# The first chunk of columns for both token tiles, unit by unit: a two-layer hybrid trunk on one core

## The chip, the core and the metric

The kernel runs on one core of a Trainium2 chip. A core has TensorE (PE: matmuls; its weight loads are shown as PEld), VectorE (DVE), ScalarE (ACT), GpSimd (POOL) and SyncE (SP, which here issues the DMAs). The metric is the device time of one execution in microseconds, the median of several runs. Before the change it is 1353.75 us, of 3 runs from 1353.36 to 1354.12.

## The reference

The input x is 256 tokens by 1024 features, float32. Two layers follow; each is a SwiGLU feed-forward, a mixing sub-layer (differential attention beside an mLSTM, gated and merged) and a second SwiGLU, each between two RMS norms:

```
h = rmsnorm(x, ffn1_norm_pre[l])
x = x + 0.5 * rmsnorm(swiglu(h, ffn1_w_gu[l], ffn1_w_down[l]), ffn1_norm_post[l])
...                                # mixing, then the second feed-forward
swiglu(h, w_gu, w_down):  g, u = split(h @ w_gu);  return (silu(g) * u) @ w_down
```

Only the very first feed-forward's first products, and the store of the last result, are touched here. Its w_gu is 1024 by 5632, its w_down 2816 by 1024.

## The kernel before, in words

**Tiling.** The tokens are two tiles of 128 (t = 0, 1). The contraction over 1024 features is eight k tiles of 128; k tiles 0 to 3 are group g = 0 and 4 to 7 are group g = 1. The columns of w_gu are taken in 11 chunks of 256 gate and 256 up columns, so one large product is 128x128 by 128x512. Every operand is in two parts, high and remainder, and a product is three matmuls (`mm3`, lines 453 to 462): high by high (L457), high of x by remainder of w (L459), remainder of x by high of w (L461). A chunk for one token tile is 8 x 3 = 24 matmuls, for both 48.

**Weights** come in units of 512 KB, [128, 1024] in SBUF; a unit of w_gu holds two k tiles of one chunk and is loaded by two DMAs of 256 KB. Units 0 to 3 are chunk 0, 4 to 7 chunk 1, 8 and 9 the first rows of w_down. `WeightStream` (lines 68 to 136) loads each into one of 5 buffers (`raw`), then splits it: a ScalarE cast (L111, `whi`) and a VectorE subtraction (L113, `wlo`), whole or in two halves of one k tile each. A unit's buffer is free for the load of the unit five later when its subtraction is done. `get` splits a unit at the latest when a product wants it; `tick` splits one more whenever PACE = 3600 ns of planned TensorE time have passed since the last tick that did so, at 216 ns for each large matmul.

**x's operand.** The first norm's weights are loaded as a row, `first_row`, and transposed to columns (L1080, L1081). For each token tile, `first` (lines 1043 to 1066) transposes x by groups of four k tiles into one PSUM bank (`transposes`, L357), multiplies the bank by the columns on VectorE (L341), casts on ScalarE (L334) and subtracts on VectorE (L336), 128x512 each. `inverse_rms` (L377, L383, L384) takes two squares on ScalarE and a power on GpSimd; its result is wanted only when a chunk is complete.

**Order.** TensorE's order is the order of the program text (`manual_schedule`). For ScalarE and VectorE the order is written only inside the block at lines 1077 to 1083, which covers token tile 0's `first`; elsewhere they, SP and GpSimd are ordered by a scheduler. `Flow` interleaves the large products with tasks: a task that waits for other engines is taken up again when a planned time has passed. In the first sub-layer `turns` gives chunk 0 as all eight k tiles of tile 0, then all eight of tile 1; tile 1's `first` is a task that begins 3000 ns of planned time after tile 0's (WAIT_FIRST). The first DMAs in SP's order: tile 0's first half, the row, tile 0's second half, units 0 to 3, tile 1 whole. When tile t of a chunk is complete, its `hidden` task (lines 502 to 513) runs: a Silu on ScalarE (L504, which brings a table load the first time), a product on VectorE (L507), two transpositions on TensorE (L511) some 18 products after the tile was complete, and a split.

`keep_busy` issues a few matmuls of nothing. PSUM has four banks `acc` (the down products' accumulators), two `mm` (a chunk's products) and two `tr` (transpositions). `new_ps` (line 492) gives a bank of `mm` when the first call covers all eight k tiles, otherwise one of `acc`.

**The end.** `Sublayer.finish` of the last sub-layer (lines 430 to 434) adds the normed result to x in two halves per token tile (L428) and stores each from SP (L433).

Of the kernel before, what the change touches and what calls it, by code (L numbers as in the profile page):

```python
# [20 lines left out]
T = 2  # L21
# [9 lines left out]
# ns of TensorE's time: a large product, a transposition; one split; what stages wait for  # L31
# [7 lines left out]
WAIT_FIRST = 3000  # L39
# [28 lines left out]
class WeightStream:  # L68
    """Weights in the order of their use: each unit of [128, 1024] is loaded, and split exactly
    into a float32r part and its float32r remainder. Loads run RAW_BUFS units ahead of the splits, the  # L70
    splits as far ahead of the products as there is room, one every PACE ns of products."""
# [27 lines left out]
    def split_parts(self, parts):  # L99
        """The next unit's split, in parts: stages"""  # L100
# [30 lines left out]
    def get(self, key, used):  # L131
        """The unit, of which a product is about to use so many elements"""
        i = self.index[key]
        self.split_to(i + 1)
        self.left[i] -= used
        return self.done[i]


class Flow:
    """The order of the instructions. The large products are the foreground; what hangs on other  # L140
    engines' results is a task, a generator that yields (its products' time, the time until its next
    stage can start), and is taken up between the large products when that time has passed."""
# [24 lines left out]
    def ran(self, n):  # L167
        """n large products have been issued."""
# [11 lines left out]
def kernel(ctx: ExitStack, tc: tile.TileContext, I, out):  # L180
# [42 lines left out]
    # k tiles a unit, and columns of a k tile  # L223
# [32 lines left out]
    x = const.tile([P, T, D], F32, name="x")  # L256
    first_row = const.tile([KD, P], F32, name="first_row")
    for hh in range(2):
        s = slice(512 * hh, 512 * hh + 512)
        nc.sync.dma_start(out=x[:, 0, s], in_=x_in[0, 0:P, s])  # L260
        if hh == 0:
            nc.sync.dma_start(out=first_row, in_=I["ffn1_norm_pre"][0].rearrange("(k p) -> k p", p=P))
    idle = w1.tile([P, 384], F32, tag="w1", name="idle")
    nc.vector.memset(idle, 0.0)
    W.load_to(4)
    nc.sync.dma_start(out=x[:, 1, :], in_=x_in[0, P:2 * P, :])
# [22 lines left out]
    def small_operands():  # L289
        """Per-feature vectors as columns, the lambdas, the gates' biases."""  # L290
# [17 lines left out]
        for l in range(L):  # L308
# [11 lines left out]
            # the negative of lambda  # L320
# [5 lines left out]
    def row(ap, nm):  # L326
        """A row vector of 1024, on every partition."""
# [4 lines left out]
    def split_out(dst_h, dst_l, src, ns):  # L332
        """Stages: src in two parts"""
# [4 lines left out]
    def columns_split_out(dst_h, dst_l, src, w, nm):  # L338
        """The same of src [128, 4, 128] times a column of w [128, 4] for each"""
# [20 lines left out]
    def transposed(src, xT, nm):  # L360
        """Stages: src [128, 1024] -> its split, transposed operand."""
# [10 lines left out]
    def squares(src, scale, nm, halves):  # L372
        """The sum of the squares of each half of src * scale"""
# [16 lines left out]
    class Sublayer:  # L390
        """What the norms between two sub-layers hold."""

        def __init__(self, i, post, pre):
            self.post_row, self.pre_row = post, pre
            self.nm = f"s{i + 1}"
            self.ahead = AHEAD if i >= 0 else 0

# [15 lines left out]
        def half(self, t, y, hh, scale):  # L413
            """y's half hh is complete."""
# [5 lines left out]
        def finish(self, t):  # L420
            """x += y * rsqrt * post; the next operand from it"""
# [8 lines left out]
            if self.pre is None:  # L430
                for s in hs:
                    update(s)
                    nc.sync.dma_start(out=out[0, t * P:(t + 1) * P, s], in_=x[:, t, s])  # L433
                return
# [18 lines left out]
    def mm3(ps, s, w, first, last):  # L453
        """ps += s.T @ w, of operands in two parts each."""
# [9 lines left out]
    def new_y(nm):  # L464
        """[128, 1024] in halves"""
        return [acc.tile([P, 512], F32, tag="acc", name=f"{nm}_{hh}") for hh in range(2)]

    def dense(y, s, w, first, last, halves=(0, 1)):
        """y += one k tile's product"""
# [4 lines left out]
    def dense_tail(ys, n, ks, operand, weights, prepare, half, finish):  # L474
        """The last k tiles, one token tile and one half after the other."""
# [8 lines left out]
    def turns(c, ahead):  # L484
        """The order in chunk c of a sub-layer: token tile, 1 for the chunk after it, k tiles. While the second token
        tile isn't there yet, the next chunk is begun."""
# [638 lines left out]
```

## Time and profile before

| | before |
|---|---|
| median of 3 runs | 1353.75 us (1353.36 to 1354.12) |
| the profiled execution: span | 1351.6 us |
| median minus span | 2.15 us |
| PE busy | 1338.9 us, 99% |
| ACT busy / DVE busy | 697.7 us, 52% / 858.7 us, 64% |
| DMA | 242.25 MB, mean 179 GB/s |

The span is from the first to the last instruction of the one profiled execution; the runs are timed from outside, which puts some 2 us around it. PE's busy time counts a matmul until a modelled end, so matmuls overlap by it; the distance between the starts of two is what one costs. [...]

### The profile page before, as it was taken

Reading aid. Unit: us, or ns where it says so; the run is one execution under the profiler, and the core shown is the slowest. Engines: PE = TensorE matmul, PEld = TensorE weight load, DVE = VectorE, ACT = ScalarE, POOL = GpSimd, SP = SyncE. Lnnn points to the kernel's source line nnn. Section 1 sums busy time; section 2 is a strip of 40 time slices with the busy share of each in tenths; the row PEclk is TensorE's granted clock in tenths of the full one; section 3 lists DMA queues with packets and bytes.
Section 4 is the critical chain, followed back from the end, with each engine's and each line's share of the span. In section 5 each row is a group of like instructions: output and inputs, shape, how many; then the busy total and the mean of one; then the engine's idle time right before and its main releaser. Section 6 shows DMA issues by size and latency. Waiting matters only on the chain.

```text
span 1351.6 us, 17400 instructions
## 1 busy us (share of the span) xinstructions
PE 1338.9 (99%) x6320; PEld 1094.8 (81%) x6320; DVE 858.7 (64%) x1245; ACT 697.7 (52%) x1063; POOL 56.2 (4%) x77
## 2 busy tenths in 40 slices
PE   8999999999999999999999999999999999999998
PEld 6888888788888888888888888887788888888886
DVE  6555566879785676555585555658887656755553
ACT  6444455567454465444464444555674444644442
POOL 1000000000000010000010000100001000100000
PEclk9999999999999999999999999999999999999999
DMA  8765659575667567555565555595664765555560
GB/s 292 246 188 187 187 156 199 147 159 118 144 187 205 175 198 228 185 186 188 180 208 185 185 186 182 164 208 122 152 161 105 206 208 174 191 184 186 186 191 32
DMA packets 160105, 242.25 MB, mean 179 GB/s; under 512 B 14250, under 2 KB 108564, under 8 KB 160020
## 3 DMA queue, kind: packets, MB, share of 16 engines
q1 hardware_dynamic: 160020, 241.15, 61.7%
q8 instruction: 49, 0.80, 0.2%
q14 instruction: 36, 0.29, 0.1%
HBM read 240.06 MB, written 1.05 MB: 178 GB/s over the span
## 4 chain that ended last, share of the span: by engine, by line
PE 94%; DVE 2%; DMA 1%; POOL 1%; issue 1%; ACT 0%; SPq 0%; DVEq 0%; POOLq 0%; ACTq 0%
PE gu L459 12%; PE gu L457 12%; PE gu L461 12%; PE y L457 6%; PE y L461 6%; PE y L459 6%; PE in_gl L461 2%; PE in_gl L459 2%; PE in_gl L457 2%; PE hp L511 1%; PE in_mv L461 1%; PE in_mv L459 1%; PE w_proj_m L457 1%; PE w_proj_a L457 1%; PE w_proj_m L459 1%; PE w_proj_a L461 1%
## 5 line engine op out<-in xcount | busy, mean ns | idle before, releaser
L113 DVE TENSOR_TENSOR wlo<-raw,whi 128x1024 fp32r<-128x1024 f32 (+2 forms) x443 | 535.8, 1217 | 254.2 <-ACT whi L111 239.4
L111 ACT CAST whi<-raw 128x1024 fp32r<-128x1024 f32 (+2 forms) x443 | 460.0, 1045 | 234.9 <-PE y L461 75.1
L459 PE MATMUL y<-wlo,hTh 128*128 128x512 f32 x352 | 142.2, 404 | 0.0
L457 PE MATMUL y<-whi,hTh 128*128 128x512 f32 x352 | 139.4, 396 | 0.0
L461 PE MATMUL y<-whi,hTl 128*128 128x512 f32 x352 | 139.2, 395 | 0.0
L457 PEld LDWEIGHTS y<-whi,hTh 128*128 128x128 f32 x352 | 66.2, 188 | 15.4
L461 PEld LDWEIGHTS y<-whi,hTl 128*128 128x128 f32 x352 | 66.4, 189 | 13.8
L459 PEld LDWEIGHTS y<-wlo,hTh 128*128 128x128 f32 x352 | 66.3, 188 | 13.7
L459 PE MATMUL gu<-wlo,x0Th 128*128 128x512 f32 x176 | 70.6, 401 | 1.0 <-DVE wlo L113 1.0
L457 PE MATMUL gu<-whi,x0Th 128*128 128x512 f32 x176 | 69.4, 394 | 1.1 <-ACT whi L111 0.7
L459 PE MATMUL gu<-wlo,s3xTh 128*128 128x512 f32 x176 | 69.7, 396 | 0.0
L459 PE MATMUL gu<-wlo,s2xTh 128*128 128x512 f32 x176 | 69.7, 396 | 0.0
L459 PE MATMUL gu<-wlo,s5xTh 128*128 128x512 f32 x176 | 69.6, 396 | 0.0
L461 PE MATMUL gu<-whi,x0Tl 128*128 128x512 f32 x176 | 69.1, 393 | 0.1
L457 PE MATMUL gu<-whi,s5xTh 128*128 128x512 f32 x176 | 68.8, 391 | 0.0
L457 PE MATMUL gu<-whi,s2xTh 128*128 128x512 f32 x176 | 68.8, 391 | 0.0
L457 PE MATMUL gu<-whi,s3xTh 128*128 128x512 f32 x176 | 68.8, 391 | 0.0
L461 PE MATMUL gu<-whi,s3xTl 128*128 128x512 f32 x176 | 68.7, 391 | 0.0
L461 PE MATMUL gu<-whi,s2xTl 128*128 128x512 f32 x176 | 68.7, 391 | 0.0
L461 PE MATMUL gu<-whi,s5xTl 128*128 128x512 f32 x176 | 68.7, 391 | 0.0
L334 ACT CAST hTh<-hp 128x256 fp32r<-128x256 f32 x88 | 32.4, 368 | 36.6 <-PE hp L511 36.6
L336 DVE TENSOR_TENSOR hTl<-hp,hTh 128x256 fp32r<-128x256 f32 x88 | 37.1, 421 | 7.3 <-ACT hTh L334 7.3
(455 smaller groups left out, 2604.3 us busy)
## 6 DMA issues: line engine op xcount, KB each, us to landing
raw<-in_ffn_w_gu_dram SPq DMA_DIRECT2D x352, 256.0 KB, 4.2
raw<-in_w_in_dram SPq DMA_DIRECT2D x124, 512.0 KB, 5.1
raw<-in_ffn_w_down_dram SPq DMA_DIRECT2D x88, 512.0 KB, 4.7
raw<-in_w_proj_a_dram SPq DMA_DIRECT2D x16, 512.0 KB, 4.0
raw<-in_w_proj_m_dram SPq DMA_DIRECT2D x16, 512.0 KB, 4.7
raw<-in_w_out_dram SPq DMA_DIRECT2D x16, 512.0 KB, 4.7
gb<-in_gate_b_dram SPq DMA_DIRECT2D x8, 256.0 KB, 5.3
raw<-in_w_in_dram SPq DMA_DIRECT2D x4, 384.0 KB, 7.0
```

The lines of the kernel that those rows point to most:

```text
L111: nc.scalar.copy(hi[:, c], raw[:, c])
L113: nc.vector.tensor_tensor(lo[:, c], raw[:, c], hi[:, c].bitcast(F32), op=ALU.subtract)
L334: nc.scalar.copy(dst_h, src)
L336: nc.vector.tensor_tensor(dst_l, src, dst_h.bitcast(F32), op=ALU.subtract)
L457: nc.tensor.matmul(ps, lhsT=sh, rhs=wh, start=first, stop=False)
L459: nc.tensor.matmul(ps, lhsT=sh, rhs=wl, start=False, stop=False)
L461: nc.tensor.matmul(ps, lhsT=sl, rhs=wh, start=False, stop=last)
L511: nc.tensor.transpose(out=pt[:, j, :], in_=hh[:, j * P:(j + 1) * P], identity=ident)
```

## The change

The first chunk of the first sub-layer gets an order of its own, `first_chunk`: a few k tiles of token tile 0, the same of tile 1, and so on, so that each unit of weights is used by both tiles before the next. It is inside a block in which ScalarE's and VectorE's order is the text's too. x is loaded in four halves, the first norm's row from ScalarE's queue. x's operand is made k tile by k tile: a ScalarE copy with a column scale (high) and one VectorE instruction for the remainder. Units 0 and 1 are split in halves between them; `first_weights` splits the next unit in halves. Both tiles' `inverse_rms` come near the end of the chunk. The last sub-layer's token tile 1 is updated and stored in four quarters, and the stores alternate between SP's and ScalarE's queues. (Comment lines and docstrings of the file are emptied; line numbers after the edits differ.)

```diff
-    for hh in range(2):
+    def x_half(t, hh):
         s = slice(512 * hh, 512 * hh + 512)
-        nc.sync.dma_start(out=x[:, 0, s], in_=x_in[0, 0:P, s])
-        if hh == 0:
-            nc.sync.dma_start(out=first_row, in_=I["ffn1_norm_pre"][0].rearrange("(k p) -> k p", p=P))
+        nc.sync.dma_start(out=x[:, t, s], in_=x_in[0, t * P:(t + 1) * P, s])
+
+    nc.scalar.dma_start(out=first_row, in_=I["ffn1_norm_pre"][0].rearrange("(k p) -> k p", p=P))
+    x_half(0, 0)
...
-    W.load_to(4)
-    nc.sync.dma_start(out=x[:, 1, :], in_=x_in[0, P:2 * P, :])
+    W.load_to(2)
+    x_half(1, 0)
+    x_half(0, 1)
+    W.load_to(3)
+    x_half(1, 1)
+    W.load_to(5)
...
-                for s in hs:
+                for i in range(4 if t else 2):
+                    n = D // (4 if t else 2)
+                    s = slice(n * i, n * i + n)
                     update(s)
-                    nc.sync.dma_start(out=out[0, t * P:(t + 1) * P, s], in_=x[:, t, s])
+                    (nc.scalar if i % 2 else nc.sync).dma_start(out=out[0, t * P:(t + 1) * P, s], in_=x[:, t, s])
...
         for c in range(NCH):
-            for t, i, ks in turns(c, sub_in.ahead):
-                gu(c + i, t, ks)
+            if c == 0 and sub_in.first_chunk is not None:
+                with tc.manual_schedule(engines={mybir.EngineType.Activation, mybir.EngineType.DVE}):
+                    sub_in.first_chunk(gu)
+            else:
+                for t, i, ks in turns(c, sub_in.ahead):
+                    gu(c + i, t, ks)
...
-    def first(t):
...
+    def first_T(t, g):
+        first_pts[t, g] = transposes(x[:, t, :], g, f"x0T{t}")
+
+    def first_split(t, g, js):
+
+        for j in js:
+            k = 4 * g + j
+            hi, lo = (z[:, k, :] for z in sub.xT[t])
+            pt, w = first_pts[t, g][:, j, :], first_cols[:, k:k + 1]
+            nc.scalar.activation(hi, pt, AF.Copy, scale=w)
+            nc.vector.scalar_tensor_tensor(lo, pt, w, hi.bitcast(F32), op0=ALU.mult, op1=ALU.subtract)
+
+    def first_weights():
+        for _ in W.split_parts(2):
+            pass
+
+    def first_chunk(gu):
+
+        gu(0, 0, range(0, 3))
+        first_T(1, 0)
+        first_split(1, 0, range(4))
+        gu(0, 0, range(3, 4))
+        first_T(0, 1)
+        first_split(0, 1, range(4))
+        gu(0, 1, range(0, 2))
+        first_weights()
+        gu(0, 1, range(2, 4))
+        first_T(1, 1)
+        first_split(1, 1, range(4))
+        gu(0, 0, range(4, 6))
+        first_weights()
+        gu(0, 1, range(4, 6))
+        for t in range(T):
+            inverse_rms(t, sub.rt, f"n0{t}")
+        W.last = flow.now
+        gu(0, 0, range(6, 8))
+        gu(0, 1, range(6, 8))
...
-        sub.tasks[0] = flow.spawn(first(0))
-        flow.need(sub.tasks[0])
+        first_pts = {}
+        first_T(0, 0)
+        first_split(0, 0, range(2))
+        first_weights()
+        first_split(0, 0, range(2, 4))
+        first_weights()
     keep_busy(WARM1)
-    sub.tasks[1] = flow.spawn(first(1), WAIT_FIRST)
-    sub.rests = sub.tasks
+    sub.tasks = sub.rests = [[True]] * T
+    sub.first_chunk = first_chunk
```

## Rows read from the trace of the kernel before

**Rows 1.** Busy time by stretches: us, each engine's busy us (instructions), PEclk, DMA share, GB/s.
```profile
0.00:24.00 24.00, 20.51 (x82) 15.37 (x83) 15.30 (x22) 16.92 (x26) 3.54 (x17) 0.93 0.91 307
24.00:190.00 166.00, 166.00 (x746) 135.79 (x745) 93.17 (x114) 79.07 (x103) 1.39 (x2) 1.00 0.64 202
```

**Rows 2.** TensorE in order of time, chunk 0: start, duration, engine, line, instruction [idle before].
```profile
6.94 0.50 PE L457 MATMUL gu<-whi,x0Th 128*128 128x512 f32 x1 [0.39 <-ACT x0Th L334]
...
10.34 0.51 PE L457 MATMUL gu<-whi,x0Th 128*128 128x512 f32 x1 [0.69 <-ACT whi L111]
11.60 0.50 PE L459 MATMUL gu<-wlo,x0Th 128*128 128x512 f32 x1 [0.76 <-DVE wlo L113]
...
14.37 1.72 PE L357 MATMUL x0T1p<-ident,x 128*128 128x128 f32 x8
...
23.98 0.40 PE L457 MATMUL gu<-whi,x0Th 128*128 128x512 f32 x1
```

**Rows 3.** TensorE in order of time: hidden transpositions, and product 62 (unit 6's remainder).
```profile
22.60 0.38 PE L511 MATMUL hp<-ident,hh 128*128 128x128 f32 x2
...
26.93 0.39 PE L459 MATMUL gu<-wlo,x0Th 128*128 128x512 f32 x1
```

**Rows 4.** Busy time by stretches of 4 us, for PEclk and GB/s.
```profile
0.00:4.00 4.00, 2.70 (x12) 2.45 (x13) 0.61 (x2) 1.28 (x1) 1.81 (x13) 1.00 0.45 138
4.00:8.00 4.00, 3.48 (x16) 2.44 (x15) 3.20 (x6) 1.61 (x3) 0.00 (x0) 1.00 0.89 252
8.00:12.00 4.00, 2.33 (x7) 1.03 (x7) 2.52 (x3) 3.42 (x8) 0.30 (x1) 1.00 1.05 353
12.00:16.00 4.00, 4.00 (x16) 3.02 (x15) 2.90 (x3) 3.70 (x7) 1.44 (x3) 0.57 1.05 376
```

**Rows 5.** SP's issues in order of time: start, duration of issuing, what.
```profile
1.17 0.37 SPq L262 DMA_DIRECT2D first_row<-in_ffn_norm_pre_dram  x1
...
1.99 5.22 SPq L96 DMA_DIRECT2D raw<-in_ffn_w_gu_dram  x8
...
9.18 0.79 SPq L329 DMA_DIRECT2D s1post<-in_ffn_norm_post_dram  x1
10.09 4.86 SPq L96 DMA_DIRECT2D raw<-in_ffn_w_gu_dram  x6
```

**Rows 6.** ScalarE in order of time: a square, unit 5's cast, table load, four casts.
```profile
10.19 0.63 ACT L377 ACTIVATE n_j<-x 128x512 bf16<-128x512 f32 x1
...
17.78 1.05 ACT L111 CAST whi<-raw 128x1024 fp32r<-128x1024 f32 x1 [0.97 <-DMA raw<-in_ffn_w_gu_dram]
...
19.37 1.28 ACT L504 ACT_TABLE_LOAD   x1
...
21.04 3.89 ACT L111 CAST whi<-raw 128x1024 fp32r<-128x1024 f32 x4
```

**Rows 7.** Lines 346, 504, 507: count, ns min/median/max, first and last start, form.
```profile
L346 ACT ACTIVATE yah<-ypt,cols x8: 679/688/692, 286.0 to 1000.3; 128x512 fp32r<-128x512 f32 x8
...
L504 ACT ACTIVATE sg<-gu,s0rt x22: 473/475/482, 20.7 to 188.4; 128x256 f32<-128x256 f32 x22
...
L507 DVE SCALAR_TENSOR_TENSOR hh<-gu,s0rt,sg x22: 474/476/484, 21.2 to 189.3; 128x256 f32<-128x256 f32 x22
```

**Rows 8.** ScalarE and VectorE in order of time: half a unit's split, a whole remainder.
```profile
5.75 0.62 ACT L111 CAST whi<-raw 128x512 fp32r<-128x512 f32 x1 [3.75 <-DMA raw<-in_ffn_w_gu_dram]
...
6.46 0.68 DVE L113 TENSOR_TENSOR wlo<-raw,whi 128x512 fp32r<-128x512 f32 x1
...
10.32 1.23 DVE L113 TENSOR_TENSOR wlo<-raw,whi 128x1024 fp32r<-128x1024 f32 x1 [0.85 <-ACT whi L111]
```

**Rows 9.** The end: VectorE's last updates; the stores' KB and median us to landing.
```profile
1347.23 1.41 DVE L428 SCALAR_TENSOR_TENSOR x<-s6yw,s6r,x 128x512 f32<-128x512 f32 x2 [0.35 <-POOL s6r L384]
...
out_dram<-x SPq DMA_DIRECT2D x4, 256.0 KB, 2.0
```

**Rows 10.** Busy time by stretches: the first mixing layer's slow one.
```profile
249.00:252.00 3.00, 3.00 (x12) 2.23 (x11) 2.80 (x7) 2.63 (x9) 0.00 (x0) 0.62 0.02 5
```

More of the change, by code (lines that the diff above doesn't have):

```diff
@@ L38 @@
 HOLD = 4700
-WAIT_FIRST = 3000
 WAIT_RMS = 1600
@@ L396, in __init__ @@
             self.ahead = AHEAD if i >= 0 else 0
+            self.first_chunk = None
         def begin(self):
@@ L1041 @@
     first_cols = const.tile([P, KD], F32, name="first_cols")
-    def first(t):
-        stages = []
-        for g in range(2):
-            pt = transposes(x[:, t, :], g, f"x0T{t}")
-            ks = slice(4 * g, 4 * g + 4)
-            yield 4 * TR_NS, 0
-            stages.append(columns_split_out(sub.xT[t][0][:, ks, :], sub.xT[t][1][:, ks, :], pt, first_cols[:, ks],
-                                            f"x0s{t}{g}"))
-            next(stages[g])
-        if t == 0:
-            w = W.split_parts(2)
-        else:
-            yield 0, 500
-        for g in range(2):
-            if t == 0:
-                next(w)
-            next(stages[g])
-            if t == 0:
-                next(w)
-            next(stages[g], None)
-        if t == 0:
-            next(w, None)
-            W.split_to(2)
-        inverse_rms(t, sub.rt, f"n0{t}")
+    def first_T(t, g):
[30 more added lines that the diff above has]
+        gu(0, 1, range(6, 8))
     for t in range(T):
```

## The prediction

> **What bounds the kernel now.** I read first the busy time by stretches, then TensorE's order of instructions in the first chunk, then the other engines' and SP's order in the same stretch. From 24 to 190 us TensorE is busy all the time at full clock [rows 1], so whatever arrives earlier there carries through to the end, and nothing gained on another engine does. The first 24 us are the exception: 3.5 us without a matmul and a mean granted clock of 0.93 [rows 1]. The first chunk of columns needs 48 large products (8 k tiles, 2 token tiles, 3 each). They start at 6.94 and the first product of the next chunk starts at 23.98 [rows 2], 17.0 us for 48 x 0.23 = 11.0 us of dense products. The 0.23 is the spacing of the 13 products from 23.98 [rows 2] to product 62 at 26.93 [rows 3]: 2.95 / 13. [...] The products of the second k pair wait for whole units of weights: 10.34 for the cast, 11.60 for VectorE's remainder [rows 2]. [...] The DMA engines are full from 8 us on, at 353 to 376 GB/s [rows 4].
>
> **The change, part by part.**
>
> *Loads.* The row of norm weights leaves SP and half of x goes behind two units, so the first weights are issued at 1.17 instead of 1.99 [rows 5]. The same bytes follow in another order; x's second tile is now in two halves of 256 KB, one behind unit 1 and one behind unit 2. Arrivals follow from the bytes of [rows 4]: 0.55 MB by 4 us, 1.56 by 8, 2.97 by 12, 4.48 by 16. Unit 5 closed 4.72 MB before (x 1.05, six units 3.15, the post-norm row 0.52), which at 376 GB/s more is 16.6 by that count, and ScalarE saw it at 17.78 [rows 6]: 1.1 us from count to use. So in the new order: first half of tile 1 (1.57 MB) 9.1, second half of tile 0 (1.84) 9.9, unit 2 (2.36) 11.4, last half of x (2.62) 12.1, unit 3 (3.15) 13.6, unit 4 (3.67) 15.0. None is later than its use below by more than 0.3.
>
> *Operands by k tile.* Before: one VectorE multiply, a cast and a subtraction for 512 columns. After: per k tile one ScalarE copy with a scale and one VectorE instruction, 128x128, 16 of each. No such instruction is in the trace. ScalarE: 128x512 with a column scale 0.688, 128x256 from PSUM with one 0.475 [rows 7]; the line through both gives 0.37 at 128, and the ends are 0.16 (the 128x512 row in four) and 0.475 (no shorter than 256). I take 0.37, as the lower end leaves no fixed part. VectorE alike, 0.476 at 256 [rows 7], ends 0.12 and 0.476; I take 0.34. ScalarE's x work becomes 16 x 0.37 = 5.9 (ends 2.6 and 7.6); VectorE's about 5.5.
>
> [...]
>
> *First products.* The transpositions of tile 0 end near 5 as before; two copies and half of unit 0 (its cast 0.62, its remainder 0.68, a whole one 1.23 [rows 8]) put the first product at about 6.2, 0.7 earlier. Unit 1, now in halves and one half-x transfer ahead of its old place (about 1 us), is cast in halves until 8.8; product 8 waits for half a remainder at about 9.0 where it waited until 11.60. Product 9 ends near 9.5.
>
> *From there TensorE has its data.* 39 products x 0.23 = 9.0, and 12 transpositions at 0.11 (the two of 22.60 lie in one product's gap plus 0.23 [rows 3]) to 0.215 (1.72 / 8 [rows 2]), 1.3 to 2.6: the chunk would end at 19.8 to 21.1, against 23.98, a gain of 2.9 to 4.2 in the chunk alone.
>
> *What is late next.* ScalarE's and VectorE's order in this stretch is now written out. Two splits come in by the pace of one per 3600 ns: unit 2 behind product 17 (17 x 216 = 3672) and unit 5 behind product 34; so the two calls written there split units 3 and 4. ScalarE's order after product 34 is: unit 5, four squares, table load, Silu of tile 0, unit 6. Behind unit 5's cast, if its load is not there, all of these queue, and then TensorE: the transpositions of chunk 0's hidden tile stand behind product 60, and product 62 wants unit 6's remainder. Unit 5's load goes into unit 0's buffer, free about 1 us earlier than before. If SP still issues the post-norm row ahead of it (9.18, unit 5 from 10.09 [rows 5]), unit 5 is seen at 17.8, as before; if not, 0.52 MB less lie ahead of it and it is seen at 16.3, and ScalarE is free for it at 16.7. From its start: cast 0.97 (3.89 / 4), squares 4 x 0.63 = 2.5, table load 1.28 [rows 6], Silu 0.48 [rows 7], unit 6's cast 1.05, remainder 1.23 [rows 8], some 0.1 of handing over: 7.6. Product 62 starts at 25.4 or 24.3, against 26.93 [rows 3]: a gain of 1.5 or 2.6. I take the middle, 2.0. Unit 7 comes behind Silu of tile 1 and its cast and remainder; a hidden tile's cast ahead of it can cost 0.4 at product 68, of which I take 0.2. So 1.8 remains of the 2.9 to 4.2.
>
> *Accumulators.* Because it is issued in pieces, chunk 0 takes two of the four banks of the down products. They are free with Silu and product of the hidden tile, near 26, and wanted some 9 us later: nothing. If that cover went, each us late is a us.
>
> *The tail.* Tile 1's last update in quarters over two queues: two of 128x512 take 1.41, then a store lands 2.0 after its issue [rows 9]. Four of 128x256 at 0.39 to 0.48 take 1.6 to 1.9, so the last issue is 0.2 to 0.5 later, of half the bytes (up to 0.6 off the landing). -0.4 to +0.5; I take -0.1. [...]
>
> **Sum.** The profiled span is 1351.6; the median of the runs 1353.75 lies 2.15 above it, which I leave unchanged. 1353.75 - 1.8 - 0.1 = 1351.85; I say 1351.8.
>
> **Rivals.**
> - A, ScalarE is full (0.10). Nothing waits for DMA but it has no gap from 4.9 on: 16 copies 5.9, eight half casts 5.0, units 2 and 5 2.1, squares 2.5, table 1.3, Silu 0.5, unit 6 1.05 = 18.4, with 1.5 of waits for units 0 and 1 until 24.8; product 62 at 26.1, gain 0.8: 1352.9. For it: the sum; against: casts overlap to 0.97 back to back.
> - B, the clock falls early (0.15). The nine products between 6 and 9.5 are still thin, and a thin stretch stands ahead of the slow one now. A stretch like that of 12 to 16, at 0.57, costs 1.7; part of it is hidden behind unit 5: gain 0.8 to 0.3, 1353.2. Against: the products are twice as close as before.
> - C, unit 5 late, slower than before (0.10). Its load falls behind both norm rows, one 0.52 MB more at 353 GB/s = 1.5, or two; ScalarE, bound to its order, stands before squares and Silu. 17.8 + 1.5 makes product 62 26.9, no gain: this decides from 19.3 on. At 20.8 it is 1.5 slower: 1355.2.
> - D, no stall follows (0.10): Silu and unit 6 are placed so that TensorE does not wait, and the chunk's 2.9 to 4.2 stay: 1350.2.
> - E, the order does not take, or the start moves with the same arrivals (0.05): 1353.7.
>
> The forecast has 0.50, its own range 1350.8 to 1352.7. A stretch at half clock in the first mixing layer (0.62 from 249 to 252 [rows 10]) may shift or vanish when work comes earlier; it can add or take about 1.5. With C and D that gives 1349.9 to 1354.5. A measurement of this kernel can tell 0.2%, 2.7 us, from no change. Below 1351.05: most of D, a quarter of the forecast, and the luck of the mixing layer: 0.29. Above 1356.45: a part of C and what I don't see: 0.06. Within: 0.65.
>
> **What would show it.** First product near 6.2 and product 9 done before 10; no clock below 1 between 12 and 16; first product of chunk 1 between 19.8 and 21.1; then a wait of 1 to 1.5 us at products 61 and 62 for unit 6, ScalarE having waited for unit 5 or run full. Wrong if chunk 1 starts at 23 or later, if ScalarE's 128x128 copies exceed 0.475, or if the first wait of TensorE after 21 us is not at unit 6.

## The result: 13 us slower, and the profile after

The changed kernel takes 1366.33 us (median of 5 runs, 1364.32 to 1368.44) against 1353.36 for the kernel before on the same chip: a ratio of 1.0092, 95% interval 1.0081 to 1.0103. The forecast was 1351.8, the range 1349.9 to 1354.5. The profiled execution has a span of 1365.1 against 1351.6, 13.5 us more, and all but 0.7 of it arises before 57 us.

The first reading is a count: the start of the n-th large product (128x512; "product n" from here on) in the changed kernel less that in the kernel before. It is +0.4 at product 1, -2.3 at product 24, +1.2 at 60, +4.7 at 62, +6.4 from 72 to 97, +12.8 at 133, and stays there to product 169. So the order does bring the chunk's first half forward by 2.3 us, and then three things take it back: one in the middle of the first chunk, one at product 61, one between products 97 and 133. The granted clock, PEclk, is a share of TensorE's full one; it reads 1.00, or 0.50 as in the kernel before from 12.40 to 15.60 us, or between where a stretch has both. The busy time by stretches has the same (us, each engine's busy us with its instructions, granted clock, DMA share, GB/s), against [rows 1, 4]:

```profile
0.00:24.00 24.00, 17.73 (x74) 13.95 (x75) 11.89 (x28) 11.72 (x26) 1.81 (x13) 0.93 0.75 244
24.00:60.00 36.00, 29.77 (x113) 23.26 (x112) 19.52 (x23) 20.05 (x32) 1.75 (x4) 0.86 0.79 254
...
8.00:12.00 4.00, 3.97 (x13) 3.06 (x14) 2.49 (x5) 1.43 (x4) 0.00 (x0) 0.57 1.01 344
...
16.00:20.00 4.00, 1.22 (x7) 0.66 (x6) 2.55 (x5) 2.98 (x6) 0.00 (x0) 1.00 0.92 306
20.00:24.00 4.00, 4.00 (x18) 3.18 (x18) 2.54 (x7) 1.94 (x5) 0.00 (x0) 1.00 0.10 20
24.00:28.00 4.00, 4.00 (x18) 3.00 (x16) 2.22 (x3) 3.98 (x11) 1.18 (x3) 1.00 0.20 56
...
48.00:52.00 4.00, 2.27 (x7) 1.88 (x8) 4.00 (x6) 2.48 (x4) 0.00 (x0) 0.62 0.96 303
```

The reader is to see three things. TensorE, always busy from 24 us on before, now stands 6.2 of the 36 us from 24 to 60. The clock is at its lower level for a part of it (0.50 from 32 to 34 and from 50 to 54 us, 0.86 on average). And from 20 to 28 us the DMA engines move 20 and 56 GB/s, where in the kernel before they moved 367 and 207. TensorE's waits, in order of time:

```profile
7.31 0.49 PE L464 MATMUL gu<-whi,x0Th 128*128 128x512 f32 x1 [1.95 <-ACT whi L110]
...
18.52 0.50 PE L464 MATMUL gu<-whi,x0Th 128*128 128x512 f32 x1 [2.02 <-ACT whi L110]
19.78 0.49 PE L466 MATMUL gu<-wlo,x0Th 128*128 128x512 f32 x1 [0.76 <-DVE wlo L112]
...
30.38 0.50 PE L464 MATMUL gu<-whi,x0Th 128*128 128x512 f32 x1 [2.33 <-ACT whi L110]
...
31.64 0.56 PE L466 MATMUL gu<-wlo,x0Th 128*128 128x512 f32 x1 [0.54 <-DVE wlo L112]
...
49.73 0.69 PE L518 MATMUL hp<-ident,hh 128*128 128x128 f32 x2 [3.36 <-DVE hh L514]
```

The first five wait for ScalarE's cast or VectorE's remainder of a unit of weights, and no load is the reason: until 34.70 ScalarE never waits for one. ScalarE in order of time says what it did instead (start, duration, what, and in brackets the idle time before and what ended it):

```profile
4.30 1.28 ACT L1063 ACT_TABLE_LOAD   x1 [4.30 <-DVE first_cols L1105]
...
12.18 0.37 ACT L1063 ACTIVATE x0Th<-x0T1p,first_cols 128x128 fp32r<-128x128 f32 x1 [1.91 <-PE x0T1p L361]
12.97 0.37 ACT L1063 ACTIVATE x0Th<-x0T1p,first_cols 128x128 fp32r<-128x128 f32 x1 [0.42 <-DVE x0Tl L1064]
13.76 0.37 ACT L1063 ACTIVATE x0Th<-x0T1p,first_cols 128x128 fp32r<-128x128 f32 x1 [0.42 <-DVE x0Tl L1064]
14.54 0.37 ACT L1063 ACTIVATE x0Th<-x0T1p,first_cols 128x128 fp32r<-128x128 f32 x1 [0.42 <-DVE x0Tl L1064]
14.81 0.36 ACT L1063 ACTIVATE x0Th<-x0T0p,first_cols 128x128 fp32r<-128x128 f32 x1
...
17.16 0.37 ACT L1063 ACTIVATE x0Th<-x0T0p,first_cols 128x128 fp32r<-128x128 f32 x1 [0.42 <-DVE x0Tl L1064]
17.43 2.07 ACT L110 CAST whi<-raw 128x1024 fp32r<-128x1024 f32 x3
...
23.06 2.08 ACT L110 CAST whi<-raw 128x512 fp32r<-128x512 f32 x3
27.62 1.28 ACT L511 ACT_TABLE_LOAD   x1
...
29.29 1.03 ACT L110 CAST whi<-raw 128x1024 fp32r<-128x1024 f32 x1
...
34.70 1.05 ACT L110 CAST whi<-raw 128x1024 fp32r<-128x1024 f32 x1 [1.85 <-DMA raw<-in_ffn_w_down_dram]
...
37.25 1.05 ACT L110 CAST whi<-raw 128x1024 fp32r<-128x1024 f32 x1 [1.23 <-DMA raw<-in_ffn_w_gu_dram]
...
42.51 1.05 ACT L110 CAST whi<-raw 128x1024 fp32r<-128x1024 f32 x1 [3.84 <-DMA raw<-in_ffn_w_gu_dram]
```

Each copy of a k tile waits for VectorE's remainder of the k tile before, and VectorE's remainders wait for the copies:

```profile
12.58 0.35 DVE L1064 SCALAR_TENSOR_TENSOR x0Tl<-x0T1p,first_cols,x0Th 128x128 fp32r<-128x128 f32 x1 [1.50 <-ACT x0Th L1063]
13.37 0.35 DVE L1064 SCALAR_TENSOR_TENSOR x0Tl<-x0T1p,first_cols,x0Th 128x128 fp32r<-128x128 f32 x1 [0.44 <-ACT x0Th L1063]
```

Both are as short as forecast, 0.37 and 0.35, but they take turns: 0.785 us a k tile. The one place without a wait is the border between two groups, where the next copy reads another transposed tile: 14.54 to 14.81, 0.27. Behind the eight copies unit 2's cast comes at 17.43, and behind four more of them unit 5's, the third of the casts from 23.06, at about 24.1. The cast at 29.29 is unit 6's, for which products 61 and 62 wait. The casts of units 7 and 8 follow from 30.59 without a wait for a load; those of units 9, 10 and 11, the last three above, wait. So the third loss begins on SP (start, duration of issuing, what):

```profile
6.81 3.44 SPq L95 DMA_DIRECT2D raw<-in_ffn_w_gu_dram  x4
10.42 0.48 SPq L333 DMA_DIRECT2D s1post<-in_ffn_norm_post_dram  x1
11.14 0.33 SPq L333 DMA_DIRECT2D s1pre<-in_mix_norm_pre_dram  x1
11.95 2.66 SPq L95 DMA_DIRECT2D raw<-in_ffn_w_gu_dram  x4
14.82 0.42 SPq L300 DMA_DIRECT2D rows<-in_conv_w_dram  x1
...
23.09 0.33 SPq L301 DMA_DIRECT2D rows<-in_conv_b_dram  x1
23.51 1.20 SPq L95 DMA_DIRECT2D raw<-in_ffn_w_gu_dram  x2
...
26.37 0.24 SPq L302 DMA_DIRECT2D rows<-in_attn_norm_w_dram  x1
...
30.15 0.38 SPq L95 DMA_DIRECT2D raw<-in_ffn_w_down_dram  x1
30.62 2.20 SPq L95 DMA_DIRECT2D raw<-in_ffn_w_gu_dram  x2
...
34.46 0.43 SPq L976 DMA_DIRECT2D gb<-in_gate_b_dram  x1
34.99 4.46 SPq L95 DMA_DIRECT2D raw<-in_ffn_w_gu_dram  x6
```

Both norm rows and twelve small loads for the mixer now stand ahead of unit 7, from 14.82 to 23.51, and that is the stretch with 20 GB/s. Unit 7 still comes in time. Five more small loads stand ahead of units 9 and 10 (30.15 and 30.62), and three more and a gate row (256 KB for the mixer) ahead of unit 11 (34.99). These are the units that ScalarE waits for, and behind the wait for unit 11 come the casts, Silu and product for which TensorE waits at 49.73.

### The profile page after: what moved, and what is told of

Read it like the earlier page. It is cut to its first block, busy times and chain, and to the rows that moved or that the text cites. A ratio compares the mean times of both kernels' runs of the same rounds, so it can differ in the third digit from the quotient of the medians.

```text
span 1365.1 us, 17426 instructions
## 1 busy us (share of the span) xinstructions
PE 1342.8 (98%) x6320; PEld 1097.1 (80%) x6320; DVE 859.5 (63%) x1258; ACT 701.0 (51%) x1078; POOL 56.2 (4%) x77
## 4 chain that ended last, share of the span: by engine, by line
PE 93%; DVE 2%; ACT 1%; DMA 1%; POOL 1%; issue 1%; SPq 0%; POOLq 0%; DVEq 0%; ACTq 0%
PE gu L466 11%; PE gu L464 11%; PE gu L468 11%; PE y L466 6%; PE y L468 6%; PE y L464 6%; PE in_gl L468 2%; PE in_gl L464 2%; PE in_gl L466 2%; PE hp L518 1%; PE in_mv L468 1%; PE in_k L464 1%; PE in_mv L466 1%; PE w_proj_m L464 1%; PE w_proj_a L464 1%; PE w_proj_m L466 1%
## 5 line engine op out<-in xcount | busy, mean ns | idle before, releaser
L464 PEld LDWEIGHTS gu<-whi,x0Th 128*128 128x128 f32 x176 | 34.2, 194 | 14.5 <-ACT whi L110 7.2
```

The source lines that it names most:

```text
L464: nc.tensor.matmul(ps, lhsT=sh, rhs=wh, start=first, stop=False)
```

## The experiments

Names that begin with a are the changed kernel with an edit, with b the kernel before with one. Each shift below is of the start of a large product against the kernel before, in us, in one profiled execution; each ratio is of runs to runs of the kernel before taken beside them. "p 24" is product 24.

| kernel | p 1 | p 24 | p 60 | p 62 | p 73 | p 169 | ratio (95%) |
|---|---|---|---|---|---|---|---|
| the change | +0.4 | -2.3 | +1.2 | +4.7 | +6.4 | +12.8 | 1.0092 (1.0081 to 1.0103) |
| a_group | -0.2 | -2.9 | -2.7 | -1.3 | -1.2 | +0.4 | 1.0005 (0.9995 to 1.0016) |
| a_banks | +2.3 | +0.9 | +1.5 | +3.7 | +5.4 | +6.8 | 1.0057 (1.0045 to 1.0070) |
| a_banks_mm | -0.2 | -1.8 | -1.2 | +1.0 | +1.5 | +2.7 | 1.0028 (1.0015 to 1.0040) |
| b_pp | +4.4 | +4.3 | +7.3 | +7.3 | +7.4 | +7.4 | 1.0048 (1.0031 to 1.0065) |
| b_ppgroup | +2.6 | -0.2 | -0.2 | -0.2 | -0.2 | -0.2 | 0.9993 (0.9984 to 1.0001) |
| a_table | -0.1 | -3.3 | +1.8 | +3.8 | +4.2 | +8.4 | 1.0059 (1.0043 to 1.0076) |
| a_sp | +0.4 | -2.1 | +4.0 | +4.9 | +5.3 | +5.3 | 1.0044 (1.0028 to 1.0060) |
| b_sp | +0.2 | -1.3 | -1.0 | -1.0 | -1.0 | +3.1 | 1.0038 (1.0024 to 1.0051) |
| a_gp | +0.4 | -2.1 | +4.0 | +7.6 | +8.0 | +8.3 | 1.0058 (1.0043 to 1.0073) |
| a_sp0 | +0.4 | -2.3 | +1.2 | +4.7 | +6.4 | +6.4 | 1.0043 (1.0030 to 1.0056) |
| b_loads | +5.2 | +2.7 | +2.9 | +2.9 | +2.9 | +2.9 | 1.0021 (1.0012 to 1.0029) |
| b_sp0 | +0.3 | -1.4 | -0.9 | -0.9 | -0.9 | +4.1 | 1.0023 (1.0014 to 1.0033) |
| a_group_table_sp | -0.7 | -4.0 | -3.8 | -2.4 | -2.3 | -2.3 | 0.9999 (0.9990 to 1.0008) |
| a_group_table_gp | -0.7 | -3.3 | +2.7 | +6.4 | +7.9 | +7.8 | 1.0044 (1.0028 to 1.0059) |
| a_group_table_sp0 | -0.7 | -4.3 | -4.1 | -1.7 | 0.0 | 0.0 | 0.9995 (0.9986 to 1.0004) |
| a_mended | -0.8 | -4.2 | -3.8 | -2.6 | -2.5 | -2.5 | 0.9993 (0.9984 to 1.0003) |

**a_group**: the copies of a call first, then its remainders.

```
-        for j in js:
+        def part(j):
...
+        for j in js:
+            hi, lo, pt, w = part(j)
             nc.scalar.activation(hi, pt, AF.Copy, scale=w)
+        for j in js:
+            hi, lo, pt, w = part(j)
             nc.vector.scalar_tensor_tensor(lo, pt, w, hi.bitcast(F32), op0=ALU.mult, op1=ALU.subtract)
```

> The kernel after, with the ScalarE copies of a call of first_split issued first and the VectorE remainders behind them, instead of alternating k tile by k tile. Theory 1 (the alternation on one PSUM bank is the cause: each k tile costs 0.79 us on both engines together, and all that comes later follows from ScalarE being behind): four k tiles take ScalarE about 1.2 us instead of 3.15, product 26 starts near 17 instead of 19.78, product 62 near 27 instead of 31.64, and the time falls by 7 to 10 us to about 1358. Rival 2 (the order of SP's loads is the cause, with small loads ahead of units 7 and on): the first 60 products come earlier but the second loss between products 97 and 133 (6.4 us) stays: about 1362. Rival 3 (the interleaved order as such, with units 5 and the squares written ahead of Silu): within 1 us of 1366.

Four copies now take 1.14 us, the turns are gone, and 12.4 of the 12.8 us with them. Product 26 starts at 15.95, product 62 at 25.62, and the time is 1354.57; all three are better than expected. The half-clock stretches behind the waits and most of the third loss went along. The granted clock reads 1.00 from 0 to 60 us, though products 3 to 7 are 0.43 apart. ScalarE of this kernel:

```profile
11.29 1.14 ACT L1066 ACTIVATE x0Th<-x0T1p,first_cols 128x128 fp32r<-128x128 f32 x4 [1.94 <-PE x0T1p L361]
12.42 1.14 ACT L1066 ACTIVATE x0Th<-x0T0p,first_cols 128x128 fp32r<-128x128 f32 x4
13.44 2.11 ACT L110 CAST whi<-raw 128x1024 fp32r<-128x1024 f32 x3
```

**a_banks** tells why they took turns: the order stays copy, remainder, copy, remainder, but a group's four transpositions are laid in two PSUM tiles.

```
-        first_pts[t, g] = transposes(x[:, t, :], g, f"x0T{t}")
+        pts = [tr.tile([P, 4, P], F32, tag="tr", name=f"x0T{t}p{g}{i}") for i in range(2)]
+        first_pts[t, g] = [pts[j % 2][:, j, :] for j in range(4)]
...
```

> The changed kernel, its copies and remainders still issued in turn k tile by k tile, but a group's four transpositions laid in two PSUM tiles (two banks): k tiles 0 and 2 in one, 1 and 3 in the other. Theory 1 (the two engines alternate because both read one PSUM bank, and the built program lets only one of them into it at a time): copy k+1 runs beside remainder k, so a k tile costs 0.40 to 0.45 us where it cost 0.79; a call of four takes some 2.0 us where it took 3.2; product 61 starts within 1 us of the run with grouped copies (24.4 us), and the time is 1353.5 to 1356. Rival 1 (they alternate because the copy writes and the remainder reads one operand tile in SBUF, x0Th, whichever bank the input is in): still 0.79 a k tile, product 61 at 30.4, time 1366. Rival 2 (VectorE's remainder is simply late, and ScalarE waits for nothing that a bank changes): the same 1366.

The first rival falls: with the operand tile in SBUF as it was, a pair of k tiles takes 0.78, 0.39 each. The time, 1361.73, missed its forecast all the same. Both tiles of the pool were now taken, so the warm-up products behind stood 3.19 us until a tile was read, product 1 came at 9.24, and the next transpositions were late too.

**a_banks_mm**: the second of the two tiles from the pool of chunk 1's accumulators (`mm`, idle until then).

> The changed kernel with copies and remainders issued in turn as it has them, a group's k tiles 0 and 2 transposed into the pool that had them and 1 and 3 into a bank of the two that chunk 1's accumulators use later, so that no tile is missing elsewhere (in the run with both tiles from the one pool a k tile cost 0.39 us, but the warm-up products behind waited for a tile until 8.36 and product 1 came at 9.24). Theory 1 (the shared bank alone makes the alternation): a k tile costs 0.40, product 1 starts at 7.3, product 61 within 1 us of the run with grouped copies (24.4), the time is 1353.5 to 1356.5. Rival (the order of instructions, copy before remainder of each k tile, costs something beside the bank): product 61 at 27 or later, 1358 and more.

Product 1 is back at 6.77, and ScalarE shows the tile (the name ends in the pool):

```profile
11.96 0.37 ACT L1067 ACTIVATE x0Th<-x0T1p0tr,first_cols 128x128 fp32r<-128x128 f32 x1 [2.94 <-PE x0T1p0tr L1059]
12.23 0.36 ACT L1067 ACTIVATE x0Th<-x0T1p0mm,first_cols 128x128 fp32r<-128x128 f32 x1
12.75 0.37 ACT L1067 ACTIVATE x0Th<-x0T1p0tr,first_cols 128x128 fp32r<-128x128 f32 x1 [0.16 <-DVE x0Tl L1068]
13.01 0.36 ACT L1067 ACTIVATE x0Th<-x0T1p0mm,first_cols 128x128 fp32r<-128x128 f32 x1
...
18.85 0.37 ACT L1067 ACTIVATE x0Th<-x0T1p1tr,first_cols 128x128 fp32r<-128x128 f32 x1 [1.19 <-DVE x0Tl L1068]
```

A copy from the other tile follows at 0.27, one from the same tile waits for its remainder (0.16 at 12.75). So the wait is one for the PSUM tile that both engines read, 0.785 us a k tile with one and 0.39 with two; the expectations call such a tile a bank. Theory 1 had the waits right and not what they are worth: product 61 came at 26.69, 2.3 us after the grouped run's, and the time 1357.43 lies above the 1356.5 expected at most, if below the rival's 1358. At 18.85 a copy still waits for a remainder that stands on VectorE behind three subtractions of weights (1.19), and a k tile costs 0.39 where it costs 0.29 in a group. Whether the hardware or the built program makes the second reader wait, no run shows.

**b_pp and b_ppgroup**: the kernel before, its order untouched, with only the operands made k tile by k tile; in b_pp in turns, in b_ppgroup grouped (the edit is the one above, in `first`).

> The kernel before, with x's operand alone made k tile by k tile as in the change (ScalarE copy, VectorE remainder, alternating, one PSUM bank per four k tiles); loads, order of products and the end as before. Theory 1: eight k tiles of tile 0 at 0.79 us each put product 13 and on behind by 2 to 3 us, and tile 1's by as much; 1356 to 1359, with a further loss if SP's order changes with it. Rival 2 and 3: within 1 us of before, 1353 to 1354.5.

> Control to the run of the kernel before with operands made k tile by k tile in turn (ratio 1.0048, 7.3 us late from product 36 on): the same with a group's four copies issued first and then its four remainders. Theory 1 (the alternation was all of that loss): within 1.5 us of before, 1353 to 1355.5. Rival (half of it is the smaller instructions, eight of them for three wide ones of 512 columns): 1357 or more.

In turns they cost 7.3 us by product 60, and the time of 1361.28 lies above the 1359 expected at most; grouped they cost nothing (0.9993). 4.4 of the 7.3 stand at product 1 already: the warm-up products waited 4.32 us for a PSUM tile that the turns held until 10.46. Grouped, the same wait is 2.76, and its 2.6 us are gone by product 24. The smaller instructions are not the price; the turns are, in the old order too.

**a_table**: a one-column ScalarE copy ahead of everything.

```
+        early = sm.tile([P, 1], F32, tag="early", name="early", bufs=1)
+        nc.scalar.copy(early, idle[:, 0:1])
         keep_busy(WARM0)
```

> The kernel after, with one ScalarE copy of a single column at the start, so that the first table load (1.28 us, at 4.30 in the trace after, behind the wait for the norm's columns) runs while ScalarE has nothing to do. Expected of all theories: the first product 1.2 us earlier, at 6.1. Theory 1: ScalarE is the engine that is behind from there on, so that all of 1.2 stays: 1365. Rival 2: SP's order decides, less than 0.5 us stays: 1366.

The table load moves from 4.30 to 1.33 and product 1 from 7.31 to 6.80, 0.5 us and not the 1.2 expected, as the first copy, at 5.59 in the change, now waits for the transpositions until 5.09. The time, 1362.52, is better than either theory's. Products 3 to 9 are at full clock here, the copies of tile 1 begin at 11.23 instead of 12.18, and this 0.95 stands at product 25 and, as 0.94, at product 62. The rest of the 4.4 us less at product 169 comes later: 1.3 between products 62 and 73, where the changed kernel has a stretch at half clock, and 2.2 in the third loss, for which no run was made. In the kernel before the table load stood at 0.72, ahead of a cast that began at 5.75; in the change ScalarE's first instruction is a copy that needs `first_cols`, and the load began when these were there.

**a_sp and b_sp**: SP's DMAs kept in the order of the program's text, after and before.

```
-    ctx.enter_context(tc.manual_schedule(engines={mybir.EngineType.PE}))
+    ctx.enter_context(tc.manual_schedule(engines={mybir.EngineType.PE, mybir.EngineType.SP}))
```

> The kernel after, with SP's issues in the order of the program text (units 5 to 10 ahead of both norm rows, the 20 small loads behind unit 20). Theory 1: up to product 62 nearly as after (31.6, at best 1 us earlier); only the second loss between products 97 and 133 goes, 6.4 us: about 1360. Rival 2 (the loads' order is the cause of all): about 1354 to 1355, product 62 near 27. Rival 3: 1365.

> Control: the kernel before with nothing changed but SP's DMAs kept in the order of the program's text. Theory 1 (before's own small loads do not delay a needed unit, so this order is worth nothing there): ratio 0.9995 to 1.0005. Rival (the order is a gain, or a loss, of its own, whatever the first chunk does): a ratio beyond 1.001 or under 0.999, and then the run of the changed kernel with this order must be read against it.

In a_sp the third loss is gone (p 73 and p 169 both +5.3). But the control is no zero: this order costs the kernel before 0.38%, 3.1 us by product 169 and 7.0 by the end of its profiled execution. So a_sp can't price the third loss by its time.

**a_gp**: the small loads issued by GpSimd; nothing else. **a_sp0 and b_sp0**: text order in the first sublayer alone.

> The changed kernel with the twenty small loads of the mixer's operands issued by GpSimd instead of SP; nothing else. Theory 1 (the second part of the loss, from product 62 to product 133, is SP's time for these small loads ahead of units 7 to 10): product 169 is 5 to 8 us later than before where it was 12.8, time 1359.5 to 1362. Rival 1 (the loads of those units are late by bytes or by buffers that come free late, not by SP's queue): product 169 still 11 us or more late, 1365 or more. Rival 2 (GpSimd, with twenty DMAs in its queue, is late with the two reciprocal roots, and the Silu behind them waits): product 62 later than 31.6.

> The changed kernel with SP's DMAs in the order of the text inside the first sublayer only. Theory 1 (two losses: alternation and table, 5 us by product 62, and SP's order, 7 to 8 us by product 133): product 169 5 us later than before, where it was 12.8, and it stays there: 1358.5 to 1359.5. Rival (the second loss follows from the lateness of the first chunk, whatever SP's order): 1363 or more.

> Control: the kernel before with SP's DMAs in the order of the text inside the first sublayer only. With that order over the whole kernel product 169 was 3.1 us late, from a wait of 2.3 us at an hp transposition and later products. Theory 1: the same 3 us late by product 169 and about 3 us in the end (1356 to 1357), since before's own order of text is a bad one for its first chunk. Rival (those 3 us came with loads of later sublayers): within 1 us of before.

From product 73 to 169 a_gp loses 0.3 and a_sp0 nothing, where the change loses 6.4: the third loss is SP's order. a_sp0 is the changed kernel to within 0.1 us up to product 73, and its splits free the buffers of units 4, 5 and 6 as late; but SP issues units 9, 10 and 11 at 25.02, 26.43 and 31.61 instead of 30.15, 30.62 and 34.99, each when its buffer comes free. So the late buffers alone cost nothing after product 73, and the small loads behind them 6.4. SP in a_sp0:

```profile
21.04 4.32 SPq L95 DMA_DIRECT2D raw<-in_ffn_w_down_dram  x2
26.43 1.20 SPq L95 DMA_DIRECT2D raw<-in_ffn_w_gu_dram  x2
...
31.61 4.46 SPq L95 DMA_DIRECT2D raw<-in_ffn_w_gu_dram  x6
```

a_gp stands 2.9 worse than the change at product 62 and 1.6 at 73. Its clock fell behind the 2.0 us pause at product 25 (last section), which cost 2.8 by product 60; but a_sp has the same fall and only 0.2 of it left at product 62. What a_gp has alone is ScalarE's wait for unit 5's load, whose cast begins at 26.95 instead of 24.09:

```profile
26.95 1.05 ACT L110 CAST whi<-raw 128x1024 fp32r<-128x1024 f32 x1 [2.53 <-DMA raw<-in_ffn_w_gu_dram]
```

Its second rival expected a late product 62 (34.49), but from GpSimd's reciprocal roots; these wait for ScalarE's squares, behind that cast. a_sp0's time, 1360.35, is above the 1359.5 expected at most, as 6.4 us and not 5 stand at product 169; its profiled execution, the longest of the five, lost another 2.4 in the first mixer. b_sp0 is 1.0023 (1.0014 to 1.0033), 4.1 us late at product 169 for 3 expected: text order suits the new order of products and not the old one.

**b_loads**: the kernel before with the change's loads alone.

> The kernel before with the change's loads alone: x's second tile as two halves between units 1 and 3, the norm row on ScalarE's queue; operands and order of products as before. Theory 1 (the loads are not the loss; x's second tile earlier delays units 2 and 3 by the 512 KB ahead of them, some 2 us, in a stretch where the old order has the TensorE wait for units anyway): 0 to 1.5 us longer, 1353.5 to 1355. Rival (the loss of 12.6 us comes with the order of the loads): 1360 or more.

The rival of 12 us falls, but 2.9 us is twice what was expected: the old order transposes all of x's first tile ahead of product 1, and its second half, now behind unit 1, held the transpositions 5.45 us and product 1 until 12.09. Loads and order belong together.

**The mended versions.** a_group_table_sp (grouped, early table, SP by text), a_group_table_gp (small loads by GpSimd instead) and a_group_table_sp0 (text order in the first sublayer) came first:

> The changed kernel with the three faults found so far mended: a call's ScalarE copies issued before its VectorE remainders, ScalarE's table load made early by a one-column copy, and SP's DMAs in the order of the program's text. Theory 1 (the losses are the alternation, the table load behind a wait and the weight loads behind small loads, and they add): from the run with grouped copies (ratio 1.0005) 1.1 us for the stall at the first hp transpositions and 0.3 to 0.5 for the table load come off: 1352.0 to 1353.2, a ratio of 0.9985 to 0.9995. Rival 1 (SP's text order costs by itself as much as it saves, since weight loads then wait behind small loads that the text puts early): 1354 to 1357, ratio over 1.0005. Rival 2 (nothing adds: time is set by the raw loads after chunk 1): equal to the grouped run within 0.3 us.

> The version put together from what the runs showed: copies grouped, table load early, SP's order left to the scheduler, small loads issued by GpSimd. Theory 1: the grouped run's products stood 2.7 us before those of before until product 60 and lost 1.1 at the first hp transpositions, where small loads stood ahead of units 7 to 10; with table and loads mended the lead of 2 to 3 us stays: 1350.5 to 1352.5, a ratio under 0.9993. Rival 1 (what SP no longer carries it fills with the gate rows of the mixer, hoisted to the same place, 256 KB each): 1353 to 1355, equal to before. Rival 2 (GpSimd late with the reciprocal roots): product 62 later than 25.6, 1354 or more.

> The changed kernel with grouped copies, the table load early, and SP's DMAs in the order of the text inside the first sublayer only; the mixer's gate rows, 256 KB each, are then hoisted to before units 6 and 8, where the grouped run had the two norm rows of 512 KB. Theory 1 (the predicted gain is there once the operands don't alternate and units 6 to 10 aren't behind other loads): product 169 stands 1.5 to 2.5 us before that of before, 0.7 of it is lost at the first mixer as in every run of the new order, and the time is 1351.3 to 1352.6, a ratio of 0.9985 to 0.9995. Rival 1 (the lead of the first chunk is always given back at the first hp transpositions): product 169 within 0.5 us of before, 1353.5. Rival 2 (the hoisted gate rows delay units 6 and 8): product 62 later than 25.6.

They gave 0.9999 (0.9990 to 1.0008), 1.0044 (1.0028 to 1.0059) and 0.9995 (0.9986 to 1.0004). The first kept a lead of 2.3 us through the first feed-forward and lost it in the mixers. In the second ScalarE waited 5.08 us for unit 5's load, as in a_gp, with GpSimd's twenty small loads beside the weights from 2.35 us on; that these are the reason was not tried apart. The third led by 4.05 at product 60 and by 0.0 at 73. Two gate rows stand ahead of units 5 and 7 in its SP order (the expectation names units 6 and 8); its unit 5 was cast 0.90 late, waiting for DMA, and the clock fell to 0.78 behind that. **a_mended** holds those rows back.

```
             b = w2.tile([P, 512], F32, tag="gb", name=f"gb{l}_{i}", bufs=2)
+            nc.vector.tensor_copy(b[:, 0:1], rt[:, 0:1])
             nc.sync.dma_start(out=b, in_=I["gate_b"][l, 512 * i:512 * i + 512].partition_broadcast(P))
```

> As the run with grouped copies, early table and SP's text order in the first sublayer, but each gate row's tile first gets a one-column write of the mixer's reciprocal root, so that its load can't be issued before the mixer. Theory 1 (the rows ahead of units 6 and 8 gave the lead back): product 62 1.5 to 2.5 us before that of before, product 169 the same, 0.7 us lost at the first mixer, time 1351.5 to 1352.8 for a before of 1353.6, ratio 0.9980 to 0.9993. Rival (the lead is lost to the chain of unit 5, the norm and Silu, whatever is loaded): product 169 within 0.6 us of before, ratio 0.9995 to 1.0010.

SP's issues in this kernel: units 3 to 9 stand in a row, with nothing between.

```profile
6.81 9.17 SPq L95 DMA_DIRECT2D raw<-in_ffn_w_gu_dram  x10
16.08 2.49 SPq L95 DMA_DIRECT2D raw<-in_ffn_w_down_dram  x2
```

TensorE, the first product and product 62:

```profile
6.12 0.51 PE L464 MATMUL gu<-whi,x0Th 128*128 128x512 f32 x1 [0.77 <-ACT whi L110]
...
24.31 0.50 PE L466 MATMUL gu<-wlo,x0Th 128*128 128x512 f32 x1 [0.54 <-DVE wlo L112]
```

Busy time by stretches, with the clock at its full level in both:

```profile
0.00:24.00 24.00, 21.24 (x94) 16.15 (x94) 14.36 (x32) 18.42 (x41) 3.60 (x17) 1.00 0.91 292
24.00:60.00 36.00, 35.69 (x161) 29.29 (x162) 22.16 (x27) 18.99 (x26) 0.00 (x0) 1.00 0.69 227
```

The lead at product 169 is the 2.5 us expected, the profiled span 1348.4, 3.2 less than before's. Another 0.9 of that comes from the first mixer, whose slow stretch this execution lacks (last section). The runs, though, go from 1350.03 to 1354.68, median 1353.32 against 1354.17, and the interval of the ratio holds 1. So the order, mended, is shown to be worth 2.5 us in one execution's first feed-forward, and not shown to beat the kernel before.

## Why the prediction was wrong, step by step

- **The step that failed: the operands by k tile.** The sum took 0.37 for ScalarE's copy and 0.34 for VectorE's remainder; they measure 0.37 and 0.35. What failed is that it counted them as two engines side by side ("ScalarE's x work becomes 16 x 0.37 = 5.9"). In turns on one PSUM tile, 16 x 0.785 is 12.6. Nothing in the rows of before showed a wait between two readers of one PSUM tile; in the old form VectorE alone read the transposed tile and ScalarE cast its copy in SBUF. The diff did show it.
- **First products.** Forecast 6.2, measured 7.31: the table load, 1.28 us, was taken as done early and moved behind a wait. With it early and the copies grouped (a_mended) product 1 starts at 6.12 and product 9 at 9.15, against a forecast end near 9.5.
- **TensorE dense from there.** Chunk 1 was to start at 19.8 to 21.1. After the change it starts at 25.16, past the 23 that the prediction named as a sign of being wrong; in a_group at 21.31, in a_mended at 20.16. The order does what the step said once the operands come in time.
- **What is late next.** The chain from unit 5's cast to product 62 was put at 7.6. It measures 7.5, from about 24.1 to 31.64. Its start was forecast at 16.7 or 17.8; the turns ahead of it in ScalarE's order made it 24.1. In a_mended, where no norm row lies ahead of unit 5, product 62 starts at 24.31, the 24.3 of that case.
- **Rival A** (0.10) had the right engine: nothing waits for a load, and ScalarE is late. But it expected ScalarE full, and it was busy 11.89 of the first 24 us; between its copies it waited for VectorE's remainders.
- **Rival C** (0.10) had the right place and sign, unit 5 late with squares, Silu and unit 6 behind it, and by its line 24.1 + 7.6 gives 31.7. Its cause was another: both norm rows did go ahead of unit 5, as it feared, but ScalarE came too late to wait for the load.
- **The clock** (rival B, with the 0.57 of [rows 4]): thin products at half clock are there, seven from 8.62 to 11.19 spaced 0.43 for 0.23. Their 1.2 us (6 x 0.20) are on the path: tile 1's transpositions stand behind product 9, and ScalarE waited 1.91 us for them until 12.18. In a_table these products are at full clock and product 25 is 0.95 earlier. So a part of this rival came true, up to 1.2 us, on top of the turns. Products 63 to 69 and those from 50 to 56 us are at half clock behind the waits of 2.3 and 3.4.
- **The stretch after the chunk.** From 24 us on "whatever arrives earlier there carries through to the end" holds for a gain (a_mended, -2.5 from product 73 on), and for a loss too where SP's order has no small loads ahead of a unit that is wanted (a_sp0, +6.4). In the change the splits free their buffers late, small loads and a gate row go ahead of units 9 to 11, and a lateness of 6.4 became 12.8. The prediction priced SP's order for unit 5 alone.
- **Accumulators**: nothing, as forecast; +6.4 at product 73 and at 97.
- **The tail**: -0.1 was taken, +0.2 measured (last updates at 1360.52 of 1365.1, 4.58 to the end, against 4.37 by [rows 9]). The quarters land 1.8 after their issue on ScalarE's queue, 0.2 less than a half's 2.0, where up to 0.6 was taken off: that 0.6 was the author's estimate, and no run shows it. With 0.2 in its place the step's own ends give 0.0 to +0.3.
- **The range** had ends for each unknown duration and none for the assumption that two engines overlap; without the turns (a_group) 12.4 of the 12.8 us are gone. Two of these ends are slips: a quarter of 0.688 is 0.17, not 0.16, and 128 columns are half of 256, which makes 0.24 of VectorE's 0.476, not 0.12. Neither enters the sum.

The three losses don't add: grouping alone takes away 12.4 us at product 169, SP's order alone 6.4, the table load alone 4.4. The third shrinks with the first: a_group, its SP order still the scheduler's, has six small loads ahead of units 9 and 10, not seventeen, issues them at 21.82 and 22.30, not at 30.15 and 30.62, and loses 1.6 from product 73 to 169, not 6.4. That fits buffers that come free earlier when the splits are on time; the scheduler's choice between them was not tried apart.

## What to carry to other kernels

When an edit splits one wide read of a PSUM tile into pieces for two engines, price the pieces in turns and not side by side, unless they lie in different tiles or one engine goes through all of them first: here a k tile took 0.785 us in turns, 0.39 from two tiles and 0.29 grouped. Where an order is written out by hand, look at what it makes the first instruction of each engine wait for, and print the order of the queues that are still planned by a scheduler: a few us of slack there were filled with small loads, and these cost as much again, 6.4 of the 12.8 us at product 169. Move the loads, the operands and the queue behind a first stretch together: the loads alone cost the kernel before 2.9 us (b_loads), and of all these runs only a_mended (-2.5) and a_group_table_sp (-2.3), which have all three, kept over 2 us of the first chunk's lead to product 169.

## What the runs showed that was not expected

- The same pause does not always bring the clock down. At product 25 TensorE stood 2.0 us in five traces. In the changed kernel and a_sp0 the granted clock was 1.00 from 20 to 24 us; in a_table it was 0.60, in a_sp and a_gp 0.50, with products 0.43 apart instead of 0.23 and 2.8 us more lost by product 60. In a_sp 0.2 of these are left at product 62, since TensorE waited for unit 6 there in any case.
- The first mixer differs from execution to execution by as much as the change was to gain. From product 800 to 1000, which the kernel before runs from 202.2 to 277.2 us, the mean granted clock is 0.98 there and in most of the traces, 1.00 in a_mended, a_sp, a_gp, a_banks and a_group_table_gp, which gain 0.9 to 1.7 us in it, and 0.96 in a_sp0 and a_group_table_sp, which lose 2.5 and 1.8; the others lose 0.3 to 1.8. The prediction's allowance for this stretch was 1.5 us either way.
- One kernel's executions differ with the clock: a_mended's three shortest, 1350.0 to 1350.2, have a mean clock of 0.999, its others, 1352.4 to 1354.7, 0.996 to 0.998. A gain of 2.5 us in a profile is no larger than that.
- Small loads held SP's queue out of proportion to their bytes: twelve, of 0.5 to 32 KB, from 14.82 to 23.51, 0.72 us apart on average, with 20 GB/s moved from 20 to 24 us. Before the first eight SP waited 4.3 us in all, 0.2 to 1.2 each, for loads issued earlier to land, as it waited 1.6 us in four places for the large loads between 8.5 and 14 us: in this stretch a small load waited for its place like a large one.
